# Attention stage of a two-layer hybrid trunk: the stick-breaking mask moved from matmuls into the scan's factors, two score rows in one bank, a shorter forget-gate chain, memory's values ahead of its queries

## The chip, the core and the metric

The kernel is written in Bass and Tile for Trainium2 and runs on one core of one chip. The metric is the time of one execution on the device, in microseconds (us). The engines that matter here are TensorE (PE in the profile, with PEld for its queue of weight loads), VectorE (DVE), ScalarE (ACT), GpSimd (POOL) and SyncE (SP), whose queue issues the transfers of the weights.

## What is computed

One sequence of 512 tokens of width 1024 goes through two layers. Each layer is a feed-forward block at half weight, a mixing block and a second feed-forward block, with a normalisation before and after each. The change touches the mixing block alone, whose reference, cut to what matters, is:

```python
proj = u @ w_in[l]
q_sb, k_sb, v_sb, q_fx, k_fx, v_fx, f_logit, q_mem = split(proj)
# stick-breaking attention, 8 heads of 64, in blocks of 128 queries
z = q @ k.T * scale
mask = key_pos[None, :] < q_pos[:, None]          # strict: a query does not see its own key
log_beta = log_sigmoid(z)
log_not = where(mask, log_beta - z, 0.0)
log_between = cumsum(log_not, reverse=True) - log_not
w = where(mask, exp(log_beta + log_between), 0.0)
o_sb = w @ v
# forgetting attention, 8 heads of 64
log_f = log_sigmoid(f_logit + b_forget[l])
c = cumsum(log_f)
z = q @ k.T * scale + c[:, None] - c[None, :]
o_fx = softmax(where(key_pos <= q_pos, z, -max)) @ v
# memory attention, 4 heads of 128, on 256 memory tokens
k_mem, v_mem = split(mem_n @ w_mem_kv[l])
o_mem = softmax(q_mem @ k_mem.T * 128 ** -0.5) @ v_mem
# each output is projected, gated by sigmoid(u @ w_gate + b_gate), summed, and projected by w_out
```

In the stick-breaking part, with s(z) = log(1 + exp(z)), the weight of a key is exp(z minus the sum of s(z) over that key and all later keys that the mask lets through). So a row needs s(z), a running sum from its right end, one subtraction and one exponential.

## The kernel before, in words

**Precision.** All products of 32-bit numbers are done as three matmuls on a high and a low part of both operands (`mm3`, lines 204 to 208). `split` (lines 177 to 190) makes the two parts: ScalarE copies the high one (line 180, or 183 with a scale), VectorE subtracts it from the source for the low one (line 181, or 184 with a scale).

**Weights.** A `Unit` is a block of weights of at most 512 KB. SyncE's queue fetches it into a ring of two buffers, "raw"; `split` turns it into a tile of the ring "wh" and one of the ring "wl", four buffers each. A pair of units (`wpair`) covers the 1024 rows of a weight for 256 columns.

**The order of the work.** The projections are jobs in a `Queue`, each with its units and a generator that issues the matmuls and yields their estimated time. Before a job starts, its units and at least the next four units in the order of the jobs are split, and a fetch is issued as soon as a "raw" buffer is free; so the order of the jobs is also the order of the transfers and of the splits. The attention heads are chains that `Queue.weave` puts between the jobs: a head yields ("pe", us) for matmuls that it has issued and ("wait", us) for a stretch in which jobs are to fill TensorE while ScalarE and VectorE work on the head. `Queue.until` and `Queue.past` run jobs up to a mark. The order that a program prints so is not yet the last one: a scheduler reorders each engine's instructions, ScalarE's and VectorE's above all, so that splits of weights, splits of projections and the operations of the heads stand interleaved in one queue on each engine. Banks for the results of matmuls are of two kinds, "z" and "mm", four each; 32-bit work tiles come from a ring of five.

**The mixing block** (`mixing`, from line 1235; jobs from line 1366). The normed input, `us_a`, is turned and split in eight pieces just before. `mem_kv` (line 1006) has by then queued the memory's keys and the first half of its values; the function that it returns queues the second half, and `mixing` calls that as `rest()` (line 1370) after the first of two query jobs. So the jobs stand in the order keys, keys, first values, first queries (tile `pqm`, the first job that reads `us_a`), second values (tile `pmv`, name mv_1), second queries, then the projections of the first stick-breaking pair. Each memory head calls `Q.until(marks["values"])` when its first waiting time is over, ahead of its transposes (`begun`, line 1187).

Four memory heads follow, then eight stick-breaking heads as four pairs with two halves, named (pair, half) below, then eight forgetting heads. Between them lie the projections of the next pair (`project`; tiles q and k), the values (`project_v`), and `merge`, which computes the gates (tiles pg and ga) and the output projections (tile pb) of the branch that is done.

**One stick-breaking head** (`stick_head`, line 1084). It takes four banks, one for each block i of 128 queries, and issues in each a bf16 matmul of an identity with a strict mask of -1e30 (line 1089), which starts the sum in the diagonal block. Then, for i = 3, 2, 1, 0, two matmuls add the scores of the block with the first (i + 1) x 128 keys, at least 256 wide (line 1098; each high part against high and low). The row's group of operations on w = (i + 1) x 128 columns is: absolute value, exponential, logarithm on ScalarE (lines 1102 to 1104), max(z, 0) + that on VectorE (line 1105), the running sum from the right (line 1107, a scan whose factor is a broadcast column of ones), the subtraction (line 1108) and the last exponential on ScalarE (line 1109). So a head has four groups of 512, 384, 256 and 128 columns, seven operations each. When all four are there and the waiting time has been filled with jobs, `transposed` (line 1074) transposes the result on TensorE (tile `pts`, line 1080; its first column of four reads all rows) and splits it, and `attend` multiplies it with the values. The forgetting heads (`fox_head`) use the same scheme with a causal mask, which has its own half of the constant tile `masks16`.

**Forget gate** (`forget_cumsum`, line 1214; the job is queued between the query and the key projection of the first forgetting pair, and so runs just ahead of head (3, 0)). It transposes the eight logits' rows to an 8 x 512 tile, takes y = -(logit + bias) on VectorE, then log(1 + exp(y)) by `log1p_exp` (exponential on ScalarE, a clamp on VectorE at line 195, logarithm on ScalarE), a maximum with y for large y (line 1226), and the running sum (line 1227). The tile `cs` receives the sum's high part twice (ScalarE, rows 0 and 64) and its low part twice (VectorE, line 1232, rows 32 and 96). `fox_pre` (line 1119) copies a forgetting head's high query part and low key part on GpSimd (lines 1124 and 1125) into the tile `qk`, one buffer with the tag "rs", and multiplies `cs` with a selector on VectorE for the second half.

## Time and profile before

| | |
|---|---|
| median of 3 runs | 2428.29 us (2422.43 to 2429.78) |
| the profiled execution, its own time | 2429.58 us |
| its span in the trace | 2427.8 us, 36744 instructions |
| granted TensorE clock, mean over the span | 0.997 |
| TensorE busy | 2392.5 us, 14471 matmuls |
| its weight loads busy | 2134.2 us |
| VectorE busy | 1870.4 us, 2500 instructions |
| ScalarE busy | 1365.0 us, 2201 instructions |
| GpSimd busy | 70.9 us, 124 instructions |
| transfers | 372.12 MB, mean 153 GB/s |
| the mixing blocks | memory heads from about 380 and 1585 us, stick-breaking heads to about 640 and 1845 us, the forgetting heads behind them |

The page sums each engine's busy time over the span. A group of instructions is a line with its engine, its operation, the tiles that it writes and reads (out<-in, their numbers left out), partitions x elements and type; then the count, the busy time, the mean of one in ns, and the idle time of the engine just before them with what released it. "ts" stands for the score work tiles of all stick-breaking heads, "zs" for their banks. In the view of waits a row says which engine's instructions waited for whose: total us, count, and the mean of one. In the timeline a row is one run of equal instructions: start, duration, engine, line, and in brackets a wait that ended just before. The windows view gives each stretch's busy time and granted clock.

### The profile page before, as it was taken

The numbers are of one execution on the slowest core, as the hardware profiler recorded it, in microseconds if no ns is written. First come the engines' busy times: TensorE is split into PE (matmuls) and PEld (weight loads), VectorE is DVE, ScalarE is ACT, GpSimd is POOL, SyncE is SP. The second block draws the span as 40 slices with busy tenths as digits, with TensorE's granted clock in tenths as the row PEclk, the third lists the DMA queues.
The fourth block names the chain that finished last, engine by engine and source line by source line (L and its number), as shares of the span: only waits on it lengthen the run. The fifth ranks groups of instructions, "written<-read, shape, count | busy, mean of one in ns | idle before, by whom it ended". The sixth has DMA issues, their size and how long they took to land.

```text
span 2427.8 us, 36744 instructions
## 1 busy us (share of the span) xinstructions
PE 2392.5 (99%) x14471; PEld 2134.2 (88%) x14471; DVE 1870.4 (77%) x2500; ACT 1365.0 (56%) x2201; POOL 70.9 (3%) x124
## 2 busy tenths in 40 slices
PE   9999999999999999999999999999999999999998
PEld 8998888888888889998899988888888888999886
DVE  8878876678776688788797788766778766887885
ACT  6555565567655555455554544655676655545544
POOL 0000000000110000000000000000001100000000
PEclk9999999999999999999999999999999999999999
DMA  6765454222223466655556655542232234576544
GB/s 235 225 195 186 157 192 138 77 72 70 79 70 113 153 203 196 213 175 177 193 187 215 198 184 173 185 118 70 71 87 75 65 129 150 190 230 196 177 158 151
DMA packets 249345, 372.12 MB, mean 153 GB/s; under 512 B 11450, under 2 KB 126162, under 8 KB 249172
## 3 DMA queue, kind: packets, MB, share of 16 engines
q1 hardware_dynamic: 249076, 369.74, 47.4%
q8 instruction: 114, 1.87, 0.3%
q14 instruction: 59, 0.48, 0.1%
q0 software_dynamic: 96, 0.03, 0.0%
HBM read 357.14 MB, written 12.58 MB: 152 GB/s over the span
## 4 chain that ended last, share of the span: by engine, by line
PE 78%; DVE 8%; DMA 7%; ACT 4%; issue 2%; SPq 0%; DVEq 0%; ACTq 0%
PE pg L206 3%; PE pg L207 3%; PE pg L208 3%; PE pdc L207 3%; PE pdc L206 2%; PE pdc L208 2%; PE pda L207 2%; PE pda L208 2%; PE pda L206 2%; PE pb L208 2%; PE pb L206 2%; PE pb L207 2%; DMA raw_da<-in_ffn_w_down_dram 1%; PE pwc0g L206 1%; PE pwc0g L207 1%
## 5 line engine op out<-in xcount | busy, mean ns | idle before, releaser
L206 PE MATMUL pg<-us_a,wh_wg 128*128 128x512 f32 x384 | 150.9, 393 | 0.0
L207 PE MATMUL pg<-us_a,wh_wg 128*128 128x512 f32 x384 | 150.0, 391 | 0.0
L208 PE MATMUL pg<-us_a,wl_wg 128*128 128x512 f32 x384 | 149.8, 390 | 0.0
L207 PE MATMUL pda<-wl_da,aha 128*128 128x512 f32 x224 | 87.5, 391 | 2.7 <-DVE wl_da L181 2.7
L207 PE MATMUL pdc<-wl_dc,ahc 128*128 128x512 f32 x224 | 87.6, 391 | 0.0
L208 PE MATMUL pdc<-wh_dc,alc 128*128 128x512 f32 x224 | 87.2, 389 | 0.0
L208 PE MATMUL pda<-wh_da,ala 128*128 128x512 f32 x224 | 87.2, 389 | 0.0
L206 PE MATMUL pda<-wh_da,aha 128*128 128x512 f32 x224 | 86.5, 389 | 0.0
L206 PE MATMUL pdc<-wh_dc,ahc 128*128 128x512 f32 x224 | 86.5, 389 | 0.0
L181 DVE TENSOR_TENSOR wl_dc<-raw_dc,wh_dc 128x1024 fp32r<-128x1024 f32 x50 | 61.1, 1222 | 32.2 <-ACT wh_dc L180 31.8
L208 PEld LDWEIGHTS pg<-us_a,wl_wg 128*128 128x128 f32 x384 | 72.4, 188 | 15.3
L206 PEld LDWEIGHTS pg<-us_a,wh_wg 128*128 128x128 f32 x384 | 72.4, 189 | 14.5
L207 PEld LDWEIGHTS pg<-us_a,wh_wg 128*128 128x128 f32 x384 | 72.4, 189 | 14.4
L180 ACT CAST wh_dc<-raw_dc 128x1024 fp32r<-128x1024 f32 x50 | 52.6, 1053 | 56.1 <-PE pdc L208 17.2
L184 DVE SCALAR_TENSOR_TENSOR wl_wg<-raw_wg,wh_wg 128x1024 fp32r<-128x1024 f32 x48 | 58.7, 1222 | 30.1 <-ACT wh_wg L183 29.8
L181 DVE TENSOR_TENSOR wl_da<-raw_da,wh_da 128x1024 fp32r<-128x1024 f32 x50 | 61.1, 1222 | 24.8 <-ACT wh_da L180 24.3
L180 ACT CAST wh_da<-raw_da 128x1024 fp32r<-128x1024 f32 x50 | 52.6, 1053 | 47.2 <-PE pda L208 19.7
L180 ACT CAST wh_uc<-raw_uc 128x1024 fp32r<-128x1024 f32 x44 | 46.2, 1049 | 50.7 <-PE pwc1u L207 10.7
L181 DVE TENSOR_TENSOR wl_uc<-raw_uc,wh_uc 128x1024 fp32r<-128x1024 f32 x44 | 53.7, 1221 | 24.7 <-ACT wh_uc L180 24.1
L180 ACT CAST wh_ua<-raw_ua 128x1024 fp32r<-128x1024 f32 x44 | 46.0, 1048 | 44.7 <-PE pwa1u L207 12.5
L181 DVE TENSOR_TENSOR wl_ua<-raw_ua,wh_ua 128x1024 fp32r<-128x1024 f32 x44 | 53.4, 1220 | 20.7 <-ACT wh_ua L180 19.9
L183 ACT ACTIVATE wh_wg<-raw_wg 128x1024 fp32r<-128x1024 f32 x48 | 51.0, 1062 | 28.2 <-PE pv L1043 16.2
(639 smaller groups left out, 8954.6 us busy)
## 6 DMA issues: line engine op xcount, KB each, us to landing
raw_da<-in_ffn_w_down_dram SPq DMA_DIRECT2D x74, 512.0 KB, 5.1
raw_dc<-in_ffn_w_down_dram SPq DMA_DIRECT2D x74, 512.0 KB, 4.8
raw_ga<-in_ffn_w_gate_dram SPq DMA_DIRECT2D x68, 512.0 KB, 4.6
raw_ua<-in_ffn_w_up_dram SPq DMA_DIRECT2D x68, 512.0 KB, 4.4
raw_gc<-in_ffn_w_gate_dram SPq DMA_DIRECT2D x68, 512.0 KB, 4.0
raw_uc<-in_ffn_w_up_dram SPq DMA_DIRECT2D x68, 512.0 KB, 4.3
raw_wg<-in_w_gate_dram SPq DMA_DIRECT2D x48, 512.0 KB, 3.6
raw_wo<-in_w_out_dram SPq DMA_DIRECT2D x24, 512.0 KB, 3.6
```

What stands on the lines that cost most here:

```text
L180: both = [nc.scalar.copy(h_ap, src)]
L181: make = lambda: nc.vector.tensor_tensor(l_ap, src, h_ap.bitcast(F32), ALU.subtract)
L183: both = [nc.scalar.activation(h_ap, src, AF.Copy, scale=scale)]
L184: make = lambda: nc.vector.scalar_tensor_tensor(l_ap, src, scale, h_ap.bitcast(F32), ALU.mult, ALU.subtract)
L206: nc.tensor.matmul(pt, lh, rh, start=start, stop=False, skip_group_check=free)
L207: nc.tensor.matmul(pt, lh, rl, start=False, stop=False, skip_group_check=free)
L208: nc.tensor.matmul(pt, ll, rh, start=False, stop=stop, skip_group_check=free)
```

## The change

There are four edits, and a fifth that follows from the first.

- **Strict mask.** The mask matmuls of the stick-breaking heads and their half of the constant tile go. A new tile `cut`, 128 x 640, made by GpSimd once per layer with the tag "rs" (the buffer that `fox_pre` uses later), holds ones, a zero on the diagonal of one block and a zero on the diagonal that is one column to the left of another. It is the factor of the scan: the running sum starts at 1e30, and the zero multiplies away what has been summed so far at the first column that the mask lets through. So the columns that are masked carry 1e30 or more in the sum, and their exponential is zero.
- **Two rows in one bank.** Rows 1 (256 columns) and 0 (128 columns, its matmul 256 wide) go into one bank, side by side, and are one group of 384 columns. A one-column `memset` of 1e30 on VectorE, between the addition and the scan, sets the sum back to 1e30 at the border between the two rows. A head has three groups of 512, 384 and 384 columns and uses three banks. The yield behind the scores is 1.4 in place of 1.5.
- **Forget gate.** ScalarE takes the absolute value with the bias, the exponential of its negative and the logarithm; VectorE takes min(logit + bias, 0) beside that, and the scan adds this and subtracts the logarithm in one pass. The clamp and the maximum go. `cs` gets one copy on ScalarE and one subtraction on VectorE; the other two parts are copied from these by GpSimd.
- **Memory's values.** `rest()` is called ahead of the loop over the query jobs, so that the second half of the values stands ahead of both query jobs.
- `stick_head` takes `cut` as an argument, and `mixing` makes it with `cuts` before the weave of the memory heads.

```diff
--- before.py
+++ after.py
@@ -92,8 +92,7 @@
     nc.vector.memset(eps_t[:], D * EPS)
     one_t = cst.tile([P, 1], F32, name="one_t")
     nc.vector.memset(one_t[:], 1.0)
-    masks16 = cst.tile([P, P + 1], BF16, name="masks16")
-    causal16, strict16 = masks16[:, 0:P], masks16[:, 1:P + 1]
+    causal16 = cst.tile([P, P], BF16, name="causal16")
     sel = cst.tile([104, NH], F32, name="sel")
 
     def tmp(name):
@@ -139,10 +138,10 @@
         later(nc.vector.tensor_copy(ident16[:], ident[:]))
 
         t0 = tmp("c0")
-        later(nc.vector.memset(t0[:, :P + 1], 0.0))
-        nc.gpsimd.affine_select(out=t0[:, 256:257 + P], in_=t0[:, :P + 1], pattern=[[-1, P + 1]], compare_op=ALU.is_ge,
+        later(nc.vector.memset(t0[:, :P], 0.0))
+        nc.gpsimd.affine_select(out=t0[:, 256:256 + P], in_=t0[:, :P], pattern=[[-1, P]], compare_op=ALU.is_ge,
                                 fill=-1e30, base=0, channel_multiplier=1)
-        later(nc.vector.tensor_copy(masks16[:], t0[:, 256:257 + P]))
+        later(nc.vector.tensor_copy(causal16[:], t0[:, 256:256 + P]))
 
         t1 = tmp("c1")
         later(nc.vector.memset(t1[:104, :8], 0.0))
@@ -1081,34 +1080,47 @@
             split(tri_part(tri, 0, kt), tri_part(tri, 1, kt), pt[:, kt * P:].rearrange("p (a b) -> p a b", b=P))
         return tri
 
-    def stick_head(q, k, vts, pj, j, ot, name):
+    CUT = NT * P + P
+
+    def cuts(name):
+
+        t = stile([P, CUT], "rs", "cut" + name, F32)
+        nc.gpsimd.memset(t[:], 1.0)
+        for c, before in ((CUT - 2 * P, 1), (CUT - P, 0)):
+            o = t[:, c - before:c + P]
+            nc.gpsimd.affine_select(out=o, in_=o, pattern=[[-1, P + before]], compare_op=ALU.not_equal, fill=0.0,
+                                    base=before - 1, channel_multiplier=1)
+        return t
+
+    def stick_head(q, k, vts, pj, j, cut, ot, name):
 
         ptile = {}
-        pzs = [pbank("z", f"z{name}_{i}") for i in range(NT)]
-        for i, pz in enumerate(pzs):
-            nc.tensor.matmul(pz[:, i * P:(i + 1) * P], ident16[:], strict16, start=True, stop=False,
-                             skip_group_check=True)
-
-        for i in reversed(range(NT)):
-            pz = pzs[i]
-            w = (i + 1) * P
-            wp = max(w, 256)
-            qs = slice(i * P, (i + 1) * P)
-            for kk in (j, 2 + j):
-                nc.tensor.matmul(pz[:, :wp], q[:, j, qs], k[:, kk, :wp], start=False, stop=(kk == 2 + j),
-                                 skip_group_check=True)
-            zr, t = pz[:, :w], tmp(f"t{name}_{i}")
+        for rows in ((3,), (2,), (1, 0)):
+            pz = pbank("z", f"z{name}_{rows[0]}")
+            w0 = (rows[0] + 1) * P
+            for i in rows:
+                o = pz[:, (rows[0] - i) * 2 * P:][:, :max((i + 1) * P, 2 * P)]
+                for kk in (j, 2 + j):
+                    nc.tensor.matmul(o, q[:, j, i * P:(i + 1) * P], k[:, kk, :o.shape[1]], start=(i == rows[0] and kk == j),
+                                     stop=(kk == 2 + j), skip_group_check=True)
+            w = w0 + (len(rows) - 1) * P
+            zr, t = pz[:, :w], tmp(f"t{name}_{rows[0]}")
 
             nc.scalar.activation(t[:, :w], zr, AF.Abs)
             nc.scalar.activation(t[:, :w], t[:, :w], AF.Exp, scale=-1.0)
             nc.scalar.activation(t[:, :w], t[:, :w], AF.Ln, bias=one_t[:])
             nc.vector.scalar_tensor_tensor(t[:, :w], zr, 0.0, t[:, :w], ALU.max, ALU.add)
-            back = t[:, w - 1::-1]
-            nc.vector.tensor_tensor_scan(back, one_t[:].broadcast_to([P, w]), back, 0.0, ALU.mult, ALU.add)
+            if len(rows) > 1:
+                nc.vector.memset(t[:, w0 - 1:w0], 1e30)
+            c1 = CUT if len(rows) > 1 else CUT - P
+            back, fac = t[:, w - 1::-1], cut[:, c1 - w:c1][:, ::-1]
+            nc.vector.tensor_tensor_scan(back, fac, back, 1e30, ALU.mult, ALU.add)
             nc.vector.tensor_tensor(t[:, :w], zr, t[:, :w], ALU.subtract)
             nc.scalar.activation(t[:, :w], t[:, :w], AF.Exp)
-            ptile[i] = t
-        yield ("pe", 1.5)
+            for i in rows:
+                c = (rows[0] - i) * 2 * P
+                ptile[i] = t[:, c:c + (i + 1) * P]
+        yield ("pe", 1.4)
         yield ("wait", W_SB0)
         wt = transposed(ptile, name)
         yield ("pe", 1.1)
@@ -1220,16 +1232,18 @@
         for t in range(NT):
             nc.tensor.transpose(pt[:NH, t * P:(t + 1) * P], fl[:, t], ident[:])
         yield 0.3
-        a, b = tmp(f"fa{l}")[:NH], tmp(f"fb{l}")[:NH]
-        nc.vector.tensor_scalar(b, pt[:NH], bfor[:, l:l + 1], -1.0, ALU.add, ALU.mult)
-        log1p_exp(a, b)
-        nc.vector.tensor_tensor(a, b, a, ALU.max)
-        nc.vector.tensor_tensor_scan(b, one_t[:NH].broadcast_to([NH, S]), a, 0.0, ALU.mult, ALU.subtract)
+        a, b, y = tmp(f"fa{l}")[:NH], tmp(f"fb{l}")[:NH], bfor[:, l:l + 1]
+        nc.scalar.activation(a, pt[:NH], AF.Abs, bias=y)
+        nc.scalar.activation(a, a, AF.Exp, scale=-1.0)
+        nc.scalar.activation(a, a, AF.Ln, bias=one_t[:NH])
+        nc.vector.tensor_scalar(b, pt[:NH], y, 0.0, ALU.add, ALU.min)
+        nc.vector.tensor_tensor_scan(b, b, a, 0.0, ALU.add, ALU.subtract)
         cs = stile([P, S], "cs", f"cs{l}")
         nc.gpsimd.memset(cs[:].bitcast(F32), 0.0)
-        for c in (0, 64):
-            nc.scalar.copy(cs[c:c + NH], b)
-            nc.vector.tensor_tensor(cs[c + 32:c + 32 + NH], b, cs[0:NH].bitcast(F32), ALU.subtract)
+        nc.scalar.copy(cs[0:NH], b)
+        nc.vector.tensor_tensor(cs[32:32 + NH], b, cs[0:NH].bitcast(F32), ALU.subtract)
+        for c in (0, 32):
+            nc.gpsimd.tensor_copy(cs[64 + c:64 + c + NH], cs[c:c + NH])
         holder["cs"] = cs
 
     def mixing(l, src, ks, vs, rest, dst):
@@ -1363,11 +1377,10 @@
             marks["gates", br] = Q.add(ug, lambda: (us_ for m in range(2) for us_ in sigmoid(m)))
             return Q.add(ub, run)
 
+        marks["values"] = rest()
         for c in range(2):
             un = wpair(w_in[l], ND, 3080 + c * 256, f"qm{l}_{c}")
             marks["qm", c] = Q.add(un, lambda c=c, un=un: q_mem(c, un), src.ready(range(NT)) if c == 0 else None)
-            if c == 0:
-                marks["values"] = rest()
         marks["first"] = marks["qm", 0]
 
         heads = [(0, p) for p in range(NP)] + [(1, p) for p in FOX]
@@ -1433,7 +1446,8 @@
                     gen = following
 
             def stick(p, j):
-                return stick_head(st["q", 0, p], st["k", 0, p], st["v", 0, p // 2], p % 2, j, st["o", 0][p], f"s{l}_{p}_{j}")
+                return stick_head(st["q", 0, p], st["k", 0, p], st["v", 0, p // 2], p % 2, j, st["cut"], st["o", 0][p],
+                                  f"s{l}_{p}_{j}")
 
             def pre(at, j):
 
@@ -1450,6 +1464,7 @@
                                 f"f{l}_{p}_{j}", lambda: pre(at, j + 1))
 
             begun, fx = {}, {}
+            st["cut"] = cuts(f"{l}")
             st["o", 0] = [blk("o", f"o{l}_0_{p}") for p in range(NP)]
             Q.weave(mems(), marks[0, 1])
             for p in range(NP):
```

## The prediction

> **What bounds the kernel now.** I read the page first, then TensorE's waits, then stages of the span in the windows view, then the timeline around each wait. Page and wait rows:
>
> ```profile
> span 2427.8 us, 36744 instructions
> ...
> PE 2392.5 (99%) x14471; PEld 2134.2 (88%) x14471; DVE 1870.4 (77%) x2500; ACT 1365.0 (56%) x2201; POOL 70.9 (3%) x124
> ```
> ```profile
> PE pts L1080 <- ACT ts L1109: 5.0, 2, 2.5
> ...
> PE pqm L206 <- ACT us_a L183: 2.7, 2, 1.7
> ...
> PE pqm L207 <- DVE us_a L184: 0.4, 2, 0.2
> ```
> ```profile
> PEld pts L1080 <- ACT ts L1109: 8.4, 8, 2.9
> ```
>
> TensorE is busy for 99% of the span, so an edit pays only if it takes matmuls away or shortens one of its waits. Two of the waits lie in what is edited. The memory queries' first matmul (pqm) waits for the normed input, once per layer. The stick-breaking heads' transposes (pts) wait for the head's last exponential, 2.5 us once per layer. The weight-load row says more: its queue waited for that exponential 8 times, so in 8 of the 16 heads the chain of exponentials and scans ends last, not TensorE's other work. In the timeline these are, in both layers, the heads (1,0), (1,1), (3,0) and (3,1) (pair, half); the other four have their last exponential 2.3 to 9.3 us early.
>
> A wait also has an echo. The windows view just behind three of them (the columns after the first are busy time of PE, PEld, DVE, ACT and POOL, each with its count; then granted clock, DMA share, GB/s):
>
> ```profile
> 380.00:384.00 4.00, 2.23 (x14) 1.55 (x12) 2.48 (x3) 2.50 (x4) 0.00 (x0) 1.00 0.41 135
> 384.00:388.00 4.00, 3.85 (x10) 3.03 (x11) 2.45 (x4) 1.05 (x1) 0.00 (x0) 0.60 0.60 144
> 1588.00:1592.00 4.00, 3.79 (x16) 2.83 (x16) 2.75 (x5) 1.76 (x3) 0.00 (x0) 1.00 0.87 245
> 1807.00:1812.00 5.00, 4.29 (x17) 3.78 (x18) 4.63 (x10) 4.02 (x10) 1.35 (x2) 0.66 0.00 0
> ```
>
> After the query wait of layer 0 the granted clock is 0.60 for 4 us: 0.40 x 4 = 1.6 us lost. After that of layer 1 it stays at 1.00. After (3,0) of layer 1 it is 0.66 for 5 us, 1.7 us lost. So a wait of 2 us or more may cost 1.6 to 1.7 us on top.
>
> **The change part by part.** All times are of the profiled execution: 2429.58 us, of which 2427.8 are its span; it lies 1.3 above the median of the runs, 2428.29.
>
> *Values ahead of queries.* The matmuls of the second half of memory's values are 2 tiles x 8 k x 3 = 48, and need no normed input. The change puts them ahead of the first query job, and their two weight units take the queries' places in SP's queue and in the split order; SP issues as many transfers as before.
>
> ```profile
> 373.44 0.28 PE L1041 MATMUL pmv<-wh_mv,mn 128*128 128x256 f32 x1
> 373.56 0.28 PE L1042 MATMUL pmv<-wl_mv,mn 128*128 128x256 f32 x1
> ...
> 383.41 1.28 DVE L184 SCALAR_TENSOR_TENSOR us_a<-uta,us_a 128x512 fp32r<-128x512 f32 x2
> 384.61 0.68 DVE L181 TENSOR_TENSOR mv<-pmv,mv 128x512 fp32r<-128x512 f32 x1
> 385.23 1.23 DVE L181 TENSOR_TENSOR wl_mv<-raw_mv,wh_mv 128x1024 fp32r<-128x1024 f32 x1
> ```
>
> They start 0.12 us apart, so there are 5.8 us of cover where the waits are. The wait rows give 2.7 + 0.4 = 3.1 us; a matmul is drawn 0.16 longer than its spacing, so each of the four hides 0.16 more: 3.7 in all, about 2.2 in layer 0 and 1.5 in layer 1. Is anything late next? In layer 0 the values begin where the wait began, about 380.8, and end at 386.6. The last normed piece is there at 384.7; the second query unit is split where the second value unit was, to 386.5, and is needed 12 matmuls of 0.227 into the queries. Neither is late: -3.7. The wait's echo in layer 0 goes with it: -1.6. What the values covered before (the first memory head's softmax) the second query job covers now, with the same TensorE time between the head's scores and its transposes (8.3 us) in the new instruction order: 0.
>
> *Strict mask out of the matmuls.* Four bf16 matmuls per head go, 64 in all; the causal ones of the forgetting heads stay.
>
> ```profile
> 453.44 0.40 PE L1089 MATMUL zs<-masks,ident 128*128 128x128 bf16 x4
> 453.64 1.55 PE L1098 MATMUL zs<-k,q 128*128 128x512 f32 x8
> ```
>
> From the first mask to the first score 0.20 us. That counts only where TensorE ends last: 8 heads x 0.20 = -1.6. In the 8 chain-bound heads it only makes the wait 0.2 longer (at most another 8 x 0.2 for the range). The new factor tile is made by GpSimd, busy 70.9 us in the whole span, once per layer and tens of us before its first reader: 0.
>
> *Two rows in one bank.* The score matmuls stay eight. Rows 1 and 0 (256 and 128 wide) become one group of 384, so a head's chain has three groups of 7 operations, not four, and one column memset. Rows of this stage, 430 to 640 us (mean ns):
>
> ```profile
> L181 DVE TENSOR_TENSOR k<-pk,k 64x512 fp32r<-64x512 f32 x12 | 8.2, 684 | 2.8 <-ACT k L180 2.7
> L1107 DVE TENSOR_TENSOR_SCAN ts<-one_t,ts 128x384 f32<-128x384 f32 x8 | 7.9, 983 | 0.0
> ...
> L1108 DVE TENSOR_TENSOR ts<-zs,ts 128x384 f32<-128x384 f32 x8 | 4.4, 546 | 0.0
> L1105 DVE SCALAR_TENSOR_TENSOR ts<-zs,ts 128x384 f32<-128x384 f32 x8 | 4.4, 544 | 0.0
> L1109 ACT ACTIVATE ts<-ts 128x384 f32<-128x384 f32 x8 | 4.2, 520 | 2.3 <-DVE ts L1108 2.2
> ...
> L1107 DVE TENSOR_TENSOR_SCAN ts<-one_t,ts 128x128 f32<-128x128 f32 x8 | 3.2, 402 | 0.0
> ```
>
> VectorE's and ScalarE's sums fall a little, but the end of the chain gets longer: the last group's scan, subtraction and exponential now take 0.98 + 0.55 + 0.52, and the transposes wait for just that group. The scheduler also fills the longer scans with other work, which now stands ahead of the last subtraction. I follow the chain in the new instruction order; an operation that follows another on VectorE starts about 0.08 after less than its duration (as in these rows), and the memset costs 0.06.
>
> ```profile
> 512.03 1.22 DVE L181 TENSOR_TENSOR wl_q<-raw_q,wh_q 128x1024 fp32r<-128x1024 f32 x1
> ...
> 516.37 0.31 ACT L1109 ACTIVATE ts<-ts 128x128 f32<-128x128 f32 x1
> ```
> ```profile
> 528.07 1.22 DVE L184 SCALAR_TENSOR_TENSOR wl_wg<-raw_wg,wh_wg 128x1024 fp32r<-128x1024 f32 x1 [0.28 <-ACT wh_wg L183]
> ...
> 536.62 0.40 DVE L195 TENSOR_SCALAR ga<-ga 128x512 f32<-128x512 f32 x1
> ...
> 538.27 0.74 DVE L201 SCALAR_TENSOR_TENSOR ga<-pg,nbgate,ga 128x512 f32<-128x512 f32 x1
> ...
> 617.90 0.68 DVE L1105 SCALAR_TENSOR_TENSOR ts<-zs,ts 128x512 f32<-128x512 f32 x1
> ...
> 623.89 1.20 DVE L181 TENSOR_TENSOR wl_wb<-raw_wb,wh_wb 128x1024 fp32r<-128x1024 f32 x1
> ```
>
> (1,0): the weight split starts at 511.7 (one add of row 1 now stands behind it), then subtraction 0.47, add 0.46, key split 0.58, memset 0.06, scan 0.87, the second key split 0.58 (it was behind the last subtraction), subtraction 0.55, exponential 0.52: with the split's 1.14 that is 5.3, an end at 517.05 in place of 516.68. +0.35. (1,1): from the split at 528.07 the new order needs 10.1 us to the last subtraction (two weight splits 2.3, a 64-row split 0.6, the chain's 6.2, and both gate operations 1.0, the 0.74 one having stood behind the chain); the exponential ends near 538.75, was 537.97. +0.8. (3,1): from 617.90 it is 7.4 to the last subtraction as before, and the exponential is 0.2 longer. +0.2. Each in both layers: +2.7. The other four heads have room for this.
>
> *Forget-gate chain.* It runs on ScalarE and VectorE just ahead of head (3,0).
>
> ```profile
> 589.36 0.42 DVE L195 TENSOR_SCALAR fa<-fa 8x512 f32<-8x512 f32 x1
> 590.56 0.68 DVE L1226 TENSOR_TENSOR fa<-fb,fa 8x512 f32<-8x512 f32 x1 [0.79 <-ACT fa L196]
> ...
> 592.00 1.21 DVE L1227 TENSOR_TENSOR_SCAN fb<-one_t,fa 8x512 f32<-8x512 f32 x1
> ...
> 594.05 1.38 DVE L1232 TENSOR_TENSOR cs<-fb,cs 8x512 fp32r<-8x512 f32 x2
> ...
> 604.32 1.31 PE L1080 MATMUL pts<-ident,ts 128*128 128x128 f32 x10 [2.52 <-ACT ts L1109]
> ```
>
> The clamp 0.42, the maximum 0.68 and the 0.79 of idle between them go, and a 0.7 addition moves behind the scan, which so ends near 590.3, not 593.2. One of two 0.69 subtractions and one ScalarE copy go to GpSimd; the key factors' multiplication moves to after the last head. ScalarE's next six operations (some 0.55 each) bring row 3's logarithm to 593.6, where VectorE's chain starts; it was 597.3. But 1.23 of weight split and two key splits (1.3) now stand inside the chain: 9.0 us to the last exponential, at 602.6, was 604.26. The transposes start 1.65 earlier, twice: -3.3, and what is left of the wait, 1.2 us, is short of those behind which the clock fell: -1.7 in layer 1.
>
> The two copies on GpSimd and the later key factors (their buffer is now held by the factor tile until the last scan) must be ready by the first forgetting scores:
>
> ```profile
> 604.48 0.74 POOL L1125 CAST qk<-k 64x512 fp32r<-64x512 f32 x1 [4.47 <-DVE k L181]
> ...
> 633.59 0.40 PE L1136 MATMUL zf<-masks,ident 128*128 128x128 bf16 x4
> ```
>
> The last scan ends near 623.7. Two copies of 0.74, a memset no longer than one and VectorE's multiplication of about 0.5 end near 626.5, 7 us before. VectorE waits for them with one query split behind it, read 30 us later: 0. If the cover went, the transposes' splits behind it would be 1 us late, per layer.
>
> The trace has no scan with a second full tensor. From below 0 (the broadcast column is an operand already, and 2.4 ns per element is twice a two-tensor subtraction's rate); from above the time of reading a second tensor is added, 1.2 ns per element from the 1.22 us split of 1024: 0.6 for row 3 and 0.46 for each 384, 1.5 us per head. I take 0, nearest to the scan's own rate.
>
> *The sum:* -3.7 - 1.6 - 1.6 + 2.7 - 3.3 - 1.7 = -9.2: 2429.6 becomes 2420.4, and against the median, 1.3 lower, 2419.
>
> The Trainium skill (VectorE: DVE Perf Modes, Rules for kernel authors) says to reduce the number of chained VectorE operations, since every one pays a pipeline flush. By that alone the merged group would shorten every chain; the rows agree that a wider operation costs less than two, and the order of the queue speaks against it. It is the first rival below.
>
> The Trainium skill (TensorE: Matmul & The Clock Gate, HAM oscillation) lets the clock fall only behind idle gaps of some 3.4 us. By it a 2.2 us wait has no echo, and the sum would be 3.3 smaller; the windows above show an echo behind 2.2 us, and the measurement decides.
>
> **The rivals.** *Fewer operations win:* ScalarE, not VectorE's queue, sets the tails, so that the chain-bound heads gain their masks and lose all their waits. For: 8.4 us of waits are there to be had. Against: the orders above. The 2.7 of new wait goes, another 1.6 of masks counts, and 2 x 1.0 more at (3,0): -9.2 - 6.3, about 2413.
>
> *The wait only moves:* the queries then wait for their weights instead, because the transfers are what this boundary waits for (512 KB units landing 4 to 5 us after issue); the values' 3.7 and the echo's 1.6 stay. Against: the split times above. -3.9: 2424.5.
>
> *The change doesn't do what it says at the heads:* the forget chain's gain is eaten by the same queue (another split ahead of the last subtraction); the 5.0 of (3,0) stay. -4.2: 2424.
>
> *Slower:* the scan slows by its second tensor. Place: the three scans of each of the 8 chain-bound heads. Price: up to 1.5 each, 12 us. It decides from 9.2 / 8 = 1.15 us per head; at the full price +2.8, and with the clock falling behind two of the longer waits +6.2: 2434. Against: the scan's rate is not that of its reads.
>
> **How the numbers follow.** Forecast 0.48 (its own range 2415 to 2423); fewer operations 0.17; the wait moves 0.12; the forget gain eaten 0.15; slower 0.08. A difference of about 0.3% (7.3 us) is what a measurement of this kernel can tell from no change: faster means under 2421. Of the forecast 0.38 lies there, all of the first rival, and little of the two in the middle (0.03): 0.58. Slower, over 2435.6, is part of the last: 0.04. The rest 0.38. The clock may also fall at a wait where it did not (1.7 each, either way). Range 2410 to 2429: it reaches from beyond the first rival to the middle ones with one such fall and the spread of the runs, and leaves out the slow scan.
>
> **What would show it.** Right: no pqm wait for us_a in either layer, and a clock of 1.00 at 384 to 388; no L1089-like matmuls and 64 fewer bf16 ones; pts waits of about 1.2 us at (3,0), and new ones of 0.6 to 1.3 at (1,0) and (1,1); the 384-wide scan at 0.98. Wrong: a pqm wait on wl_qm or raw_qm, a scan above 1.1 us, a forgetting score that waits for qk, or (3,0) waiting 2.5 us still.

## The result and the profile after

The changed kernel takes 2417.64 us (median of 7 runs, 2416.4 to 2418.86), the kernel before 2425.84 us on the same chip (7 runs, 2422.43 to 2429.78): a ratio of 0.9969, 95% interval 0.9958 to 0.9979. The forecast was 2419, the range 2410 to 2429. In a later session the two stood at 2427.64 and 2430.61 us, ratio 0.9986 (0.9976 to 0.9995). So the change gains, but the size of its gain differs by 5 us between the two sessions; the last part of this section shows a part of the reason.

The profiled execution took 2418.79 us (2429.58 before). Its page, then TensorE's waits, then the weight loads' waits (total us, count, and the longest one: the third number of a wait row is not the mean, as the section on the time before has it):

```profile
span 2416.7 us, 36492 instructions
...
PE 2383.0 (99%) x14407; PEld 2128.3 (88%) x14407; DVE 1866.4 (77%) x2462; ACT 1357.7 (56%) x2137; POOL 80.9 (3%) x134
```
```profile
PE pts L1079 <- ACT ts L1119: 8.5, 8, 2.1
```
```profile
PEld pts L1079 <- ACT ts L1119: 11.8, 8, 2.5
```

The wait of the memory queries (pqm) is gone from the list in both layers. The transposes of the stick-breaking heads (pts) wait longer than before: 8.5 us in 8 places, against 5.0 in 2. The windows view at the memory queries and behind the transposes of head (3,0), layer 0 and layer 1 (columns as before: busy time by engine, granted clock, DMA share, GB/s):

```profile
380.00:384.00 4.00, 4.00 (x36) 4.00 (x35) 3.83 (x5) 2.51 (x4) 0.00 (x0) 1.00 0.47 126
384.00:388.00 4.00, 4.00 (x32) 3.87 (x32) 1.42 (x2) 1.96 (x2) 0.00 (x0) 1.00 0.48 140
596.00:600.00 4.00, 1.92 (x11) 1.30 (x10) 3.34 (x6) 2.00 (x4) 1.06 (x1) 1.00 0.11 37
600.00:604.00 4.00, 4.00 (x17) 3.42 (x15) 3.03 (x6) 2.70 (x7) 0.00 (x0) 0.57 0.00 0
1798.00:1803.00 5.00, 4.25 (x24) 3.69 (x25) 3.43 (x8) 3.98 (x8) 0.00 (x0) 1.00 0.01 2
```

TensorE is busy throughout at 380 to 388 us, at full clock. Behind the wait at (3,0) the clock falls in layer 0, where it had not before, and stays up in layer 1, where it had fallen.

**Where the time went.** The timelines give the borders of two stretches per layer: from the first transposes of the normed input (uta) to the first projection of values (pv), which holds the memory keys, values and queries; and from there to the first matmul of the output projection (pwo), which holds all other heads. Layer 0 of the kernel before, then of the changed one:

```profile
358.82 0.60 PE L564 MATMUL uta<-ident,fa 128*128 128x128 f32 x4
...
434.87 0.28 PE L1041 MATMUL pv<-wh_v,us_a 128*128 128x256 f32 x1
...
825.12 0.39 PE L206 MATMUL pwo<-wh_wo,ms 128*128 128x512 f32 x1
```
```profile
359.32 0.27 PE L563 MATMUL uta<-ident,fa 128*128 128x128 f32 x1
...
431.08 0.28 PE L1040 MATMUL pv<-wh_v,us_a 128*128 128x256 f32 x1
...
822.36 0.39 PE L205 MATMUL pwo<-wh_wo,ms 128*128 128x512 f32 x1
```

The first stretch takes 76.05 us before and 71.76 after, the second 390.25 and 391.28. From each I take off what stretches of half clock cost in it (matmuls that start 1.55 to 3.3 times their usual distance apart for over 1.5 us; the excess over the usual distance is the cost). "Full-clock time" below is what is left, for layer 0 / layer 1:

| kernel | memory stretch | heads stretch | half-clock stretches in the whole trace |
|---|---|---|---|
| before | 74.65 / 74.01 | 390.25 / 390.21 | 3, 4.5 us |
| changed | 71.77 / 71.77 | 389.66 / 389.67 | 1, 1.6 us |
| changed, later session | 71.77 / 71.77 | 389.57 / 389.60 | 5, 9.1 us |

At full clock the change so gains 2.9 + 2.2 = 5.1 us in the memory stretches and 0.6 + 0.5 = 1.1 in the heads, 6.2 in all, and the same again to 0.1 us in the later session. What differs between the two profiled executions of the changed kernel is the number of half-clock stretches: 7.5 us of the 8.8 between their spans (2416.7 and 2425.5). Over all runs it is less clear: the mean granted clock of the changed kernel is 0.9983 in the first session and 0.9962 in the later one, and 0.0021 of 2420 us is 5 of the 10 us between the two medians; the rest is open. Of the 10.8 us between the profiled executions of before and after, 6.2 are these gains, 1.4 is a half-clock stretch in layer 0's memory stretch that went, the clock behind (3,0) adds nothing in sum (1.65 in layer 1 before, 1.62 in layer 0 after), and 3.1 lie outside the change, of them 1.5 in a half-clock stretch at 890 us.

### The profile page after: what moved, and what is told of

The parts are those of the page before. It is cut to its first block, busy times and chain, and to the rows that moved or that the text cites. A ratio compares the mean times of both kernels' runs of the same rounds, so it can differ in the third digit from the quotient of the medians.

```text
span 2416.7 us, 36492 instructions
## 1 busy us (share of the span) xinstructions
PE 2383.0 (99%) x14407; PEld 2128.3 (88%) x14407; DVE 1866.4 (77%) x2462; ACT 1357.7 (56%) x2137; POOL 80.9 (3%) x134
## 4 chain that ended last, share of the span: by engine, by line
PE 83%; DVE 8%; DMA 4%; ACT 4%; issue 2%; DVEq 0%; SPq 0%; ACTq 0%
PE pg L205 3%; PE pg L206 3%; PE pg L207 3%; PE pda L206 3%; PE pda L207 3%; PE pda L205 3%; PE pdc L206 3%; PE pdc L207 3%; PE pdc L205 3%; PE pb L207 1%; PE pb L205 1%; PE pb L206 1%; PE pwa1u L205 1%; PE pwa1u L206 1%; PE pwa1u L207 1%
## 5 line engine op out<-in xcount | busy, mean ns | idle before, releaser
L180 DVE TENSOR_TENSOR wl_dc<-raw_dc,wh_dc 128x1024 fp32r<-128x1024 f32 x50 | 61.1, 1223 | 30.3 <-ACT wh_dc L179 29.8
L180 DVE TENSOR_TENSOR wl_da<-raw_da,wh_da 128x1024 fp32r<-128x1024 f32 x50 | 61.1, 1223 | 25.4 <-ACT wh_da L179 25.0
```

The lines of the kernel that those rows point to most:

```text
L180: make = lambda: nc.vector.tensor_tensor(l_ap, src, h_ap.bitcast(F32), ALU.subtract)
```

## The experiments

The main theory, from the two traces: the values cover their wait; the masks gain where TensorE ends last; the merged group of two rows makes the chain's end later; and the forget-gate chain's gain is lost to the queues of ScalarE and VectorE. Rivals: fewer operations win, or cover alone would have done it. The twelve kernels ran in three groups of four, each group beside runs of the kernel before on the same chip (medians 2430.05, 2430.11 and 2430.61 us). The wait at a head is the start of its first transpose less that of the matmul ahead, less this matmul's usual distance; heads without a column have none, or 0.1 at most (in e7 0.1 to 0.4 at the third pair).

| kernel | median us | ratio to before (95%) | memory stretch | heads stretch | (1,0) | (1,1) | (3,0) | (3,1) |
|---|---|---|---|---|---|---|---|---|
| before | | 1 | 74.65 / 74.01 | 390.25 / 390.21 | 0 | 0.23 | 2.69 / 2.67 | 0.28 |
| e1_values | 2427.02 | 0.9986 (0.9977 to 0.9996) | 71.77 / 71.77 | 390.32 / 390.33 | 0 | 0.24 | 2.66 / 2.71 | 0.29 |
| e2_forget | 2428.28 | 0.9992 (0.9983 to 1.0001) | 74.38 / 74.27 | 389.92 / 389.58 | 0 | 0.24 | 2.23 / 1.92 | 0.29 |
| e3_heads | 2432.97 | 1.0010 (1.0001 to 1.0019) | 73.07 / 74.83 | 391.18 / 391.05 | 0.90 | 0.82 | 3.79 / 3.63 | 0.90 |
| e4_mask | 2423.87 | 0.9972 (0.9962 to 0.9981) | 74.45 / 72.92 | 388.33 / 388.33 | 0 | 1.08 | 2.04 / 1.96 | 0.57 |
| e5_rest_no_merge | 2424.65 | 0.9980 (0.9971 to 0.9988) | 71.77 / 71.77 | 389.13 / 388.71 | 0 | 1.07 | 2.81 / 2.34 | 0.56 |
| e6_copy_dve | 2425.55 | 0.9984 (0.9975 to 0.9993) | 71.77 / 71.77 | 389.65 / 389.36 | 0.91 | 0.82 | 2.23 / 1.97 | 0.90 |
| e7_wait | 2425.42 | 0.9985 (0.9975 to 0.9995) | 71.77 / 71.77 | 389.13 / 389.67 | 0 | 0 | 0 | 0 |
| e8_before_wait | 2434.64 | 1.0018 (1.0008 to 1.0027) | 74.59 / 73.65 | 392.26 / 392.22 | 0 | 0 | 0 | 0 |
| e9_gate_early | 2423.21 | 0.9970 (0.9959 to 0.9981) | 71.77 / 71.77 | 390.35 / 390.11 | 0.90 | 0.83 | 1.50 / 1.49 | 0.90 |
| e10_no_merge_early | 2421.49 | 0.9962 (0.9947 to 0.9977) | 71.77 / 71.77 | 389.04 / 389.04 | 0 | 1.08 | 1.47 / 1.47 | 0.56 |
| e11_after (changed) | 2427.64 | 0.9986 (0.9976 to 0.9995) | 71.77 / 71.77 | 389.57 / 389.60 | 0.91 | 0.83 | 2.24 / 2.12 | 0.90 |
| e12_no_merge_old | 2423.21 | 0.9970 (0.9959 to 0.9982) | 71.77 / 71.77 | 388.46 / 389.01 | 0 | 1.07 | 2.14 / 2.64 | 0.56 |

**Each edit alone.** e1 takes the kernel before and only moves `marks["values"] = rest()` ahead of the loop.

> The kernel before with the values' job ahead of the queries alone. Theory (cover): the wait of 1.87 + 0.48 us in layer 0 and of 1.1 + 0.48 in layer 1 goes, with about 0.16 more for each of the four matmuls: -3.7 to -4.2, and -5.5 to -6 with the half-speed stretch behind the wait of layer 0. Matched matmul by matmul, everything behind the memory queries starts 3.8 to 6 us earlier, and the rest stands as in the kernel before (2.5 us of wait at head (3,0) in both layers). Rival (the wait only moves to the queries' weights): a new wait at the queries on their split, -1.5 or less.

The memory stretch is 71.77 us in both layers, as in the changed kernel, and the heads are as before: the theory holds, and the queries' weights are in time. The median gains 3.0 us, less than the 5.1 at full clock but inside its interval (1.0 to 5.6).

e2 takes the kernel before with the new `forget_cumsum`.

> The kernel before with the new forget-gate chain alone. Theory (ScalarE's queue): in the changed kernel's trace ScalarE stood idle for 1.4 us until the running sum was there, because the copy of that sum now stands ahead of head (3,0)'s first absolute value; it stands there in this kernel too. So the shorter chain gains only 0.5 to 1.0 us at (3,0) in each layer: a wait of 1.5 to 2.1 us in place of 2.5, time -1 to -2. Rival (the prediction): the wait falls by 1.65 per layer to below 1.0 and no half-speed stretch follows: -3.3 to -5. Second rival (no gain at all): -0.3 to +0.3.

The wait at (3,0) falls by 0.5 and 0.75 us, and the heads stretch by 0.3 and 0.6. The prediction's 1.65 is out; the median cannot tell this from nothing.

e3 has both edits of the heads, e4 the mask alone: the loop over groups of e4 is

```diff
-        for rows in ((3,), (2,), (1, 0)):
+        for rows in ((3,), (2,), (1,), (0,)):
```

> The kernel before with the strict mask in the scan's factors and the two shortest rows in one bank; the old forget-gate chain and the old place of the values. Theory: 0.30 us per head for the masks where TensorE ends last (8 heads, -2.4), and a longer end of the chain where it ends last: (1,0) +0.6, (1,1) +0.1 to 0.3, (3,1) +0.35 net of the mask, (3,0) unknown (0 to +0.8), each in two layers: -0.5 to +1.0 in all. Rival (fewer operations win): the chain-bound heads gain their 0.3 as well: -4.8 or more. Second rival (masks alone count 0.2): up to +2.

> As the run with the heads' edits alone, but with four groups and four banks per head, no memset between two rows: only the mask moves into the scan's factors. Theory (the merged group is what makes the chain's end later): waits at (1,0), (1,1) and (3,1) as in the kernel before plus the 0.3 us that TensorE comes earlier, so they cost nothing and gain nothing; the eight other heads gain 0.30 each: -2.4, that is 1.5 to 3 us less than the run with the merged group. Rival (merging costs nothing, the queue's new order does it): the same time as the merged run within 0.7 us, with the same waits at (1,0) and (1,1) of 0.8 to 0.9.

This is the clearest pair: the mask alone gains 1.9 us of heads stretch per layer and is 6.2 us faster than the kernel before; with the merged group on top the heads are 0.9 slower than before, and so is the median, by 2.9. Merging costs 2.8 us per layer here, by the waits: 0.9 at (1,0), 1.7 at (3,0), 0.3 at (3,1), and 0.3 back at (1,1). Both sizes missed their theories. e3's heads are 1.8 us longer in the two layers together, above the theory's +1.0 and inside the second rival's +2, though the masks are worth the 0.30 per head that the theory has (next section). e4's gain 3.8, not 2.4, since the wait at (3,0) also falls, by 0.65 and 0.71 us; why the mask alone does that is open. The transposes at (3,0) of e3, then those of e4:

```profile
601.68 2.39 PE L1079 MATMUL pts<-ident,ts 128*128 128x128 f32 x10 [3.63 <-ACT ts L1119]
```
```profile
601.66 1.84 PE L1079 MATMUL pts<-ident,ts 128*128 128x128 f32 x10 [1.88 <-ACT ts L1119]
```

That both stand at the same time in their traces is chance; TensorE has waited 1.75 us longer in e3 (3.63 against 1.88 in brackets). So the rival that fewer operations win is out.

What makes the merged chain end later is for the most part not its wider last group. The end of VectorE's part of head (1,0), in e3 and then in e4:

```profile
509.14 0.55 DVE L1112 SCALAR_TENSOR_TENSOR ts<-zs,ts 128x384 f32<-128x384 f32 x1
509.61 0.67 DVE L180 TENSOR_TENSOR k<-pk,k 64x512 fp32r<-64x512 f32 x1
510.23 0.06 DVE L1114 MEMSET ts<- 128x1 f32 x1
510.33 0.96 DVE L1117 TENSOR_TENSOR_SCAN ts<-cut,ts 128x384 f32<-128x384 f32 x1
511.32 0.69 DVE L180 TENSOR_TENSOR k<-pk,k 64x512 fp32r<-64x512 f32 x1
512.05 0.56 DVE L1118 TENSOR_TENSOR ts<-zs,ts 128x384 f32<-128x384 f32 x1
```
```profile
511.83 0.61 DVE L1112 SCALAR_TENSOR_TENSOR ts<-zs,ts 128x256 f32<-128x256 f32 x2
512.36 1.00 DVE L1117 TENSOR_TENSOR_SCAN ts<-cut,ts 128x256 f32<-128x256 f32 x2
513.27 0.60 DVE L1118 TENSOR_TENSOR ts<-zs,ts 128x256 f32<-128x256 f32 x2
513.78 0.67 DVE L180 TENSOR_TENSOR k<-pk,k 64x512 fp32r<-64x512 f32 x1
```

With four groups the two short ones alternate and the key splits (k) come behind them; with the merged group the scheduler puts both key splits between its operations. Counted from the head's first absolute value, the last exponential ends 1.53 us later in e3, and the two splits take 1.35 of that (from their starts to the next operation's). At (3,0) of layer 0 it is 1.54 us, and a key split and a gate operation (ga) between the merged group's operations take 1.30. At (3,1) nothing new stands there, and the wider group alone costs 0.3. This is read from the order in the traces; no run keeps the merged group and moves the splits.

**The rest without the merged group.** e5 is the changed kernel with the same edit of the loop.

> The changed kernel without the merged group: four groups and four banks per head, everything else as changed. Theory (the merged group makes the last link of the chain longer, and that is paid in the chain-bound heads): the waits of the transposes at (1,0) and (3,1) fall from 0.9 to below 0.4 us, that at (3,0) from 2.1 to 1.5 or less; time 2 to 5 us below the changed kernel, 10 to 13 below the kernel before. Rival (merging is free once the forget-gate chain is short): the same as the changed kernel within 1 us. Second rival (fewer operations win): 1 to 3 us slower than the changed kernel.

As expected at (1,0); at (3,1) the wait falls, but to 0.56 and not below 0.4; the heads stretch is 0.5 and 1.0 us shorter. Not as expected at (3,0), where the wait is longer (2.81 and 2.34). The median is 3.0 us below that of e11 on the same chip, as expected, and 5.5 below the kernel before, not 10 to 13. What the new chain does here is read against e12, which differs from e5 in the chain alone: the wait at (3,0) is 0.67 us longer with it in layer 0 and 0.30 shorter in layer 1, and so is the heads stretch. The same short chain takes 0.45 to 0.75 off the wait in the kernel before; from e3 to the changed kernel, which also has the values ahead, the wait falls by 1.4 to 1.5. So its worth hangs on what stands around it in the queues.

**What holds (3,0) up.** The changed kernel's ScalarE and VectorE ahead of (3,0) (start, duration, and in brackets the idle time that ended just before and what ended it):

```profile
584.95 0.58 ACT L1069 COPY ss<-pvs 64x512 f32<-64x512 f32 x1
586.93 0.62 ACT L1243 CAST cs<-fb 8x512 fp32r<-8x512 f32 x1 [1.40 <-DVE fb L1240]
587.46 0.59 ACT L1109 ACTIVATE ts<-zs 128x512 f32<-128x512 f32 x1
588.07 0.62 ACT L179 CAST o<-ss 64x512 fp32r<-64x512 f32 x1
...
589.62 0.72 ACT L1111 ACTIVATE ts<-ts,one_t 128x512 f32<-128x512 f32 x1
```
```profile
584.96 0.69 DVE L183 SCALAR_TENSOR_TENSOR q<-pq,q 64x512 fp32r<-64x512 f32 x1 [0.18 <-ACT q L182]
585.68 1.21 DVE L1240 TENSOR_TENSOR_SCAN fb<-fb,fa 8x512 f32<-8x512 f32 x1
586.93 0.69 DVE L1070 TENSOR_TENSOR ss<-pvs,ss 64x512 f32<-64x512 f32 x1
...
592.23 1.20 DVE L180 TENSOR_TENSOR wl_q<-raw_q,wh_q 128x1024 fp32r<-128x1024 f32 x1
...
595.75 0.68 DVE L180 TENSOR_TENSOR k<-pk,k 64x512 fp32r<-64x512 f32 x1
...
597.79 0.69 DVE L180 TENSOR_TENSOR k<-pk,k 64x512 fp32r<-64x512 f32 x1
```

ScalarE waits 1.40 us for the running sum, since its copy into `cs` stands ahead of (3,0)'s first absolute value. e6 gives that copy to VectorE:

```diff
-        nc.scalar.copy(cs[0:NH], b)
+        nc.vector.tensor_copy(cs[0:NH], b)
```

> The changed kernel with the one copy of the forget gate's running sum on VectorE and not on ScalarE. Theory (ScalarE's queue holds head (3,0) up): without the 1.4 us in which ScalarE waits for the sum, the first absolute value of (3,0) starts 1.2 to 1.8 us earlier, the wait of its transposes falls from 2.1 to 0.6 to 1.2 us in each layer and no half-speed stretch follows: 2 to 3 us below the changed kernel. Rival (VectorE's queue holds it up): the copy's 0.4 to 0.7 us on VectorE stand ahead of the head's first addition, the wait stays at 2 us or more, time the same within 0.5.

The theory falls; the rival, VectorE's queue, holds: the wait is 2.23 and 1.97 us, against 2.24 and 2.12 in e11. ScalarE does both first absolute values and exponentials early now, and then waits just as long one step later:

```profile
589.67 0.62 ACT L179 CAST o<-ss 64x512 fp32r<-64x512 f32 x1 [1.50 <-DVE ss L1070]
590.32 0.72 ACT L1111 ACTIVATE ts<-ts,one_t 128x512 f32<-128x512 f32 x1
```

The copy of the last head's output (o) stands ahead of (3,0)'s logarithm, and it waits for a sum (ss) that VectorE makes only behind the forget gate's operations. e9 takes the whole job out of the way, beside head (2,1), which has 3.1 us to spare:

```diff
                 Q.add(un, lambda: v_gates(br, p // 2, un))
+                Q.add([], lambda: forget_cumsum(l, st["fl"], st))
...
-                if (br, p, x) == (1, FOX[0], "q"):
-                    Q.add([], lambda: forget_cumsum(l, st["fl"], st))
```

> The changed kernel with the forget-gate job queued right behind the projection that makes the logits, one job earlier, so that it runs beside head (2,1), whose chain ends 3.1 us early, and no longer ahead of (3,0). Theory (VectorE's queue: the chain's operations stand ahead of the last head's output sum, for which ScalarE waits before (3,0)'s first logarithm): the wait of the transposes of (3,0) falls from 2.25 to below 1.2 us in each layer, 1 to 4 us below the changed kernel; in exchange TensorE may wait for the logits' copy up to 1 us. Rival (the head's own chain of three wide groups sets it): the wait stays above 1.8 us, the time the same within 1.

The wait at (3,0) falls from 2.25 to 1.50, less than expected: the gate's place accounts for 0.75 us. The rest is, by the order in the trace, the head's own chain and the splits in it, which no run tests. And the exchange is bad at full clock, since TensorE now waits for the logits' copy at the gate's transposes:

```profile
573.26 0.38 PE L1233 MATMUL pfl<-ident,fl 128*8 128x128 f32 x2
575.32 0.27 PE L1233 MATMUL pfl<-ident,fl 128*8 128x128 f32 x1 [0.97 <-DVE fl L1284]
```

The heads stretch is 0.4 to 0.8 us longer than in the changed kernel, and yet the median is 4.4 lower. The profiled executions show one possible reason: no half-clock stretch at (3,0) in e9, one in each layer in e11, its neighbour on the chip (1.7 and 1.6 us; see the last section). But these two executions are only 0.9 us apart (2426.73 and 2427.64), e9's being 3.5 above its own median, so most of the 4.4 is not seen in them.

**Cover alone.** e7 and e8 plan 2.5 us more waiting time for the heads of the second and fourth pair, in the changed kernel and in the kernel before, which puts 11 or 12 more matmuls between the scores and the transposes of the second pair's heads and 6 more in those of the fourth:

```diff
-        yield ("wait", W_SB0)
+        yield ("wait", W_SB0 + (2.5 if late else 0.0))
```

> The changed kernel with 2.5 us more waiting time planned for the heads of the second and fourth pair, so that 12 more matmuls (2.7 us) stand ahead of their transposes. Theory (the chain's end is what TensorE waits for, and there is other work to put there): the 8 waits of 8.5 us in all go, and the half-speed stretch of 1 us behind (3,0): 6 to 9 us below the changed kernel. Rival (the work is then missing behind the transposes, where TensorE waits for the split of the transposes or for the next head's scores): the time the same within 1.5 us, with new waits at the products with the values or at the projections.

> The kernel before with the same 2.5 us more of planned waiting time for the heads of the second and fourth pair, nothing else. Theory: the 2.5 us waits at (3,0) go, with the half-speed stretches that follow some of them: 4 to 7 us below the kernel before; so most of what the forget-gate chain was to gain could be had by cover alone. Rival (the work is then missing later): within 1.5 us of the kernel before.

The waits at these heads' transposes go, all of them, and a wait of 3 us per layer appears where the rival has it, at a head's product with the values (e7's timeline, layer 0):

```profile
606.18 0.68 PE L1066 MATMUL pvs<-pts,v 128*128 128x512 f32 x1 [3.04 <-ACT pts L179]
```

At full clock e7's heads gain 0.5 us in layer 0 and nothing in layer 1; e8 loses 2.0 per layer. The work moved ahead is missing behind. e8's median is 4.5 us above the kernel before, outside both of its expectations, and e7's is 2.2 below that of e11 on the same chip, where its theory has 6 to 9.

**Together.** e10 has four groups and the gate's job early; e12 has the mask with four groups, the values ahead, and the old chain; e11 is the changed kernel beside them.

> Four groups and four banks per head, with the strict mask in the scan's factors, the new forget-gate chain one job earlier, the values ahead of the queries. Theory (the merged group costs at (1,0) and (3,1), the gate's place at (3,0)): the waits of the transposes are 0 at (1,0), 1.1 at (1,1), below 1.2 at (3,0) and 0.6 at (3,1); 3 to 7 us below the changed kernel. Rival (TensorE waits for the logits or for the next head in its place): within 1.5 us of the changed kernel.

> The changed kernel as it is, beside the others on one chip: 8 us below the kernel before, 6 to 11 with the half-speed stretches that come and go; waits of the transposes of 0.90, 0.83, 2.25 and 0.89 us at (1,0), (1,1), (3,0) and (3,1) as in its first trace.

> Two edits alone: the strict mask in the scan's factors with four groups and four banks, and the values ahead of the queries; the forget-gate chain as before. Theory (the merged group and the new chain bring nothing beside these two): the stretch from the values' projection to the first forgetting score takes 197.0 to 197.5 us in each layer without half-speed stretches, against 198.4 to 199.0 in the changed kernel, and 71.8 us from the first transposes of the normed input to there as in the changed kernel: 2 to 4 us below the changed kernel. Rival (the short chain is needed): 1 us or more above the changed kernel.

The waits of e10 are as expected but for (3,0), at 1.47. It is the fastest of the three, 6.1 us below the changed kernel and 9.1 below the kernel before; only 1.1 of the 6.1 are heads stretch at full clock. Its clock behind (3,0) stays at 1.00:

```profile
PE pts L1079 <- ACT ts L1119: 5.3, 6, 1.3
```
```profile
598.00:602.00 4.00, 4.00 (x22) 3.39 (x21) 3.23 (x6) 2.99 (x6) 0.00 (x0) 1.00 0.00 0
602.00:606.00 4.00, 4.00 (x22) 3.44 (x21) 1.85 (x3) 2.26 (x3) 0.20 (x1) 1.00 0.41 131
```

e11 gains 3.0 us on the kernel before, less than I expected, with the waits of its first trace. e12 is 4.4 us below it, without the merged rows and without the short chain. From the values' projection to the first forgetting score it takes 197.2 and 197.8 us at full clock, against 198.3 and 198.4 in e11. So the expectation holds but for layer 1, 0.3 us above its 197.0 to 197.5: beside the mask and the values, the two other edits as they stand in the changed kernel bring nothing.

## Why the prediction was right, and where it was not

The time came out 1.4 us below the forecast, but the terms do not all stand behind it.

- *Values ahead, -3.7: right in mechanism, too small.* It is 5.1 at full clock (2.9 and 2.2); e1 alone has the same 71.77 us. Measured from start to start, the two waits of each layer are 1.87 + 0.48 and 1.10 + 0.48 us, 3.9 in all; the other 1.2 are shorter delays around them, of 0.3 us at most. The rest of the traces with the old order spread between 72.92 and 74.83, so the wait itself varies by 2 us.
- *Its echo, -1.6: right in this pair* (1.4 by the distances). It is not sure: of the layer 0 waits of 1.75 to 1.92 us in before, e2, e4 and e8, three of four had one; in the steps of the last section, these three have 2.09, 2.03 and 2.04 us of idle time in one step, and e4's has 1.96.
- *Masks, -1.6: right in mechanism, a third too small.* A head's scores take 1.59 us with the masks before, from 453.44 to the next projection, and 1.29 after:

```profile
453.44 0.40 PE L1089 MATMUL zs<-masks,ident 128*128 128x128 bf16 x4
453.64 1.55 PE L1098 MATMUL zs<-k,q 128*128 128x512 f32 x8
455.03 0.39 PE L206 MATMUL pq<-us_a,wh_q 128*128 128x512 f32 x1
```
```profile
449.64 1.45 PE L1104 MATMUL zs<-k,q 128*128 128x512 f32 x8
450.93 0.40 PE L205 MATMUL pq<-us_a,wh_q 128*128 128x512 f32 x1
```

  So 0.30 per head, not 0.20: the first score behind the bf16 matmuls is late too. In 8 heads that is 2.4.
- *The longer tails, +2.7: right in sum, not in place.* Net of the mask's 0.30 the chain's end moved by 0.6 at (1,0), 0.3 at (1,1) and 0.3 at (3,1), 2.4 in two layers; forecast 0.35, 0.8 and 0.2.
- *The forget chain, -3.3: this step failed.* The wait at (3,0) fell from 2.69 to 2.25; with the mask that is 0.74 per layer, -1.5. The step had the scan end at 590.3, which is 586.1 in the changed kernel (4.2 us ahead there), and ScalarE's next six operations follow on. The trace has the scan's end at 586.9, 0.8 later, and ScalarE standing still for 1.40 us until then. And e12 against e5 shows that beside the mask and the values, without the merged group, the new chain loses in one layer (0.67 us) and gains in the other (0.30).
- *Clock behind (3,0) in layer 1, -1.7: it went there and came in layer 0.* Nothing in sum. The wait did not become "short of those behind which the clock fell".

The heads' terms (-1.6, +2.7, -3.3 and the clock's -1.7) summed to -3.9; the heads gave -1.1 at full clock and 0 from the clock. That the total still fits comes from the values and from 3.1 us outside the change, by which this one pair of executions differs: the closeness of the total is luck. The rivals: the waits of the queries did not move to their weights; fewer operations did not win (e3 against e4); that the forget chain's gain is eaten by the queue is near what happened. The slow scan is out:

```profile
L1117 DVE TENSOR_TENSOR_SCAN ts<-cut,ts 128x384 f32<-128x384 f32 x16 | 15.2, 947 | 0.1
...
L1117 DVE TENSOR_TENSOR_SCAN ts<-cut,ts 128x512 f32<-128x512 f32 x8 | 9.8, 1223 | 0.3
```

```profile
L1107 DVE TENSOR_TENSOR_SCAN ts<-one_t,ts 128x512 f32<-128x512 f32 x8 | 9.7, 1216 | 0.1
```

The first fence is the changed kernel's, the second that of before, both from the groups of the heads' stage. With a full second tensor the scan takes 947 ns for 384 columns and 1223 for 512; with the broadcast column 983 and 1216.

The Trainium skill (VectorE: DVE Perf Modes, Rules for kernel authors) says to keep the count of chained VectorE operations low. By that the merged group, which makes one chained operation of two, should have helped. From e4 to e3 VectorE's busy time does fall, from 1872.0 to 1870.7 us, and ScalarE's from 1365.6 to 1358.9, while the median rises by 9.1 us, 5.6 of them heads stretch at full clock: the other work that stands between the merged group's operations outweighs the operations saved. The prediction had this mechanism, with the second key split inside the chain, and priced it too low at (1,0), 0.35 against 0.6.

## What to carry to other kernels

Where TensorE waits for the end of a chain, what stands ahead of the chain's last operation in its engine's queue sets the wait: merging two links saves operations and can lose time, if the scheduler fills the longer ones with other work; so read the new order, and try each edit of a bundle alone. An engine's queue couples what the program does not: shortening one chain only lets the next operation in the queue be what is waited for, until the whole job stands somewhere else. Work that does not need the input that TensorE waits for, put ahead of that input's first use, is the sure gain here.

## What the runs showed of the hardware that I had not expected

- *Which waits are followed by half clock.* In the fourteen traces (from 30 us on, without the last 15), TensorE's waits of 0.6 to 1.5 us, start to start, were followed by a half-clock stretch in none of 184 cases, those of 1.5 us or more in 52 of 92. One stretch lasts 3.41 us, or twice that in seven places, and costs 1.3 to 2.9 us.

  It looks like chance, but the trace's record of the clock shows a rule behind it. In each trace the starts of these stretches lie whole multiples of 3.413 us apart: in e11 they are at 599.66, 886.38, 1214.06, 1804.56 and 2091.28 us, the last four 84, 180, 353 and 437 such steps behind the first. So I cut each trace into these steps and summed TensorE's idle time in each (every start-to-start distance over 0.1 us longer than usual for its shape, less the usual). Of the 9691 steps at full clock, those with 2.0 us or more of idle time were followed by half clock in 51 of 51 cases, those with 1.9 to 2.0 in 1 of 9, all others in none. With 0.05 or 0.15 us in place of the 0.1 the border blurs by 0.1 to 0.2, no more.

  The changed kernel shows it at (3,0), where it waits 2.25 us in both layers. In layer 0 the wait lies within one step, and the clock falls in the next; in layer 1 the border of two steps cuts it into 2.00 (just under) and 0.25, and the clock stays up (the steps are the windows, layer 0 and then layer 1):

```profile
597.01:600.42 3.41, 1.32 (x10) 0.90 (x9) 2.48 (x5) 1.70 (x4) 1.06 (x1) 1.00 0.00 0
600.42:603.83 3.41, 3.41 (x13) 2.83 (x12) 2.71 (x6) 2.29 (x6) 0.00 (x0) 0.50 0.00 0
...
1795.09:1798.50 3.41, 1.57 (x7) 0.95 (x6) 3.32 (x6) 1.43 (x3) 1.06 (x1) 1.00 0.09 32
1798.50:1801.91 3.41, 3.16 (x19) 2.81 (x20) 1.86 (x3) 2.57 (x7) 0.00 (x0) 1.00 0.01 2
```

  What is left to chance is where a step begins in an execution. So a wait of 2.2 us costs its length and, if nearly all of it lies in one step, 1.6 us more, as in both layers of e11; one of 1.5 us, as at (3,0) in e9 and e10, is not followed by half clock unless 0.5 us more of idle time lies in its step. That a cut from 2.2 to 1.5 us is so worth more than its 0.7 would explain a part of what e9 and e10 gain: the mean granted clock of their runs is 0.9972 in both, against 0.9962 in e11, which is 2.4 of 2425 us. It was not tried by itself.

  The Trainium skill (TensorE: Matmul & The Clock Gate, HAM oscillation) puts the fall behind gaps of more than about 3.4 us; here 2.0 us of idle time within one step are enough, and the measurement decides.
- *Eight rows on GpSimd take as long as 64.* The forget gate's copies of 8 rows and a head's copies of 64 rows and the same width have nearly the same mean in the changed kernel's rows:

```profile
L1246 POOL CAST cs<-cs 8x512 fp32r<-8x512 f32 x2 | 2.1, 1070 | 2.7 <-ACT cs L1243 2.6
L1136 POOL CAST qk<-q 64x512 fp32r<-64x512 f32 x2 | 2.1, 1064 | 12.6 <-DVE ts L1117 11.1 <-PE zf L1156 1.4
```

  Both means hide a spread. The 8-row copies took 1.12 and 1.02 us, the 64-row ones 1.52 and 0.61. In e10 the second 8-row copy took 0.61 us in each layer, and 0.61 is also what most of the 64-row copies take, there, in the changed kernel and in the kernel before; so the number of rows does not set the time, and a copy that takes longer is held up by something that the trace does not name. The prediction put 0.74 for a copy.
